# Neighbourhood attention of an encoder trunk on Trainium2: heads taken one by one, or two at a time in the halves of the TensorE array

## The chip, the cores and the metric

One core of a Trainium2 chip (trn2) runs the whole kernel. The metric is the device time of one execution in microseconds (us), median of several runs. Everything is float32. The large products are made from three matmuls in the `float32r` form (a value is cut into a high and a low part); the small products of the attention are plain float32 matmuls, each of which appears in the trace as two passes (two weight loads and two matmuls).

## What is computed

A trunk of two layers over 512 tokens of width 1024. Each layer is half a SwiGLU feed-forward step, a mixer of two groups of heads side by side, and another half feed-forward step. The part that is changed is the neighbourhood attention, eight heads of width 64 on an 8 x 64 grid of tokens:

```python
for j in range(GRID_W // COL_BLOCK):          # four blocks of 16 columns
    qb = q[:, :, :, j * COL_BLOCK:(j + 1) * COL_BLOCK]
    kb = k[:, :, :, c0:c0 + COL_SLAB][:, :, key_rows]      # 32 columns of keys
    vb = v[:, :, :, c0:c0 + COL_SLAB][:, :, key_rows]
    s = jnp.einsum('bhrqd,bhrwkd->bhrqwk', qb, kb).astype(jnp.float32) * scale
    s = s + bias[None].astype(jnp.float32)
    s = jnp.where(valid[:, None, :], s, NEG_INF)
    p = jax.nn.softmax(s.reshape(B, H, rows, COL_BLOCK, wh * COL_SLAB), axis=-1)
    outs.append(jnp.einsum('bhrqwk,bhrwkd->bhrqd', p, vb))
...
na_o = rmsnorm(merge_heads(na_o), na_gain)
```

Beside it, four heads of gated linear attention (GLA) run over the same tokens. Their outputs and those of the neighbourhood attention go through one output projection.

## The kernel before, in words

Activations lie transposed: 128 rows of features by 512 tokens per tile. A head of 64 features fills half of the 128 rows, so a pair of heads `hp` shares one tile for q and one for k. For each block `j` of 128 queries there are 256 keys.

The mixer (`mixer`, L530) is made of four streams of steps: the two GLA pairs (`gla_all`), the neighbourhood attention (`na_all`, L890) and the fillers (`fillers`, L916), which are the projections with the large weights and the first part of the output projection. `interleave` (L502) puts the steps in order by a plan: each step says how long it holds TensorE and how long its successor must wait. The order of that plan is the priority; a scheduler then takes, engine by engine, the first instruction that is ready and has its buffers, so neighbouring steps can mix.

`na_unit` (L828) is one head and two query blocks; there are 16 units in a mixer and two mixers. A unit has three steps, and `na_all` runs them staggered: in each round it begins a unit, makes the second step of the unit before and the third step of the one before that, and then waits until the planned period `NAP` = 5.46 is over.

1. Scores (L846): two matmuls of 64 rows by 256 keys, in one PSUM bank of the tag `sc`. VectorE adds the bias and takes the maximum (L851), changes its sign (L854), ScalarE makes the exponential and the sum (L855), VectorE the reciprocal (L857) and the product with it (L860). The result lies in a tile `pp`.
2. Four transposes (L864) into the PSUM bank `tp`, and a copy by ScalarE back into `pp` (L866).
3. Values (L874): four matmuls of 128 rows by 64 columns into one half, `b` to `b + 64`, of the bank `o`. After the last unit of a pair VectorE copies the bank to a tile `nao` (L879), which is split into high and low parts (`osplit`), and its squares are summed.

The bias of a head is loaded on GpSimd's DMA queue at the head's first unit (L834, L835) into two tiles `nb` of the tag `na`, which has six buffers. `pp`, `nao`, `sq` and the tiles of the row scale have the same tag.

PSUM has eight banks: four `mm` for the projections, two `sc`, which the scores of the GLA streams use as well (L623, L697, L711, L564), one `tp` and one `o`.

Of the kernel before, what the change touches and what calls it, by code (L numbers as in the profile page):

```python
# [31 lines left out]
WARM = 13  # L32
NAP = 5.46
DEPTH = 2
# [26 lines left out]
def trunk_kernel(ctx, tc, xin, wgu, wdn, win, wcode, wgate, wout, vec, rpbt,  # L61
# [42 lines left out]
    def pair(name, gain=None, src=None):  # L104
        # both parts of a tile side by side
        t = sp.tile([P, 2, T], F32R, tag="pr", name=nm(name), bufs=NPR)
        h, l = t[:, 0, :], t[:, 1, :]
        split(src, h, l, gain)
        return h, l
# [19 lines left out]

    # the tensor engine's clock comes up while the first data are on their way  # L130
    zero = cp.tile([P, P], F32, name="zero")
# [37 lines left out]

# [1 line left out]
    XC = [None] * KP  # L171
# [27 lines left out]

# [1 line left out]
    XD = [None] * KD  # L201
# [35 lines left out]
    def rsqrt_row(ps, n, t, r, a, act=False):  # L237
        # 1/sqrt(mean + eps): exp(-ln/2) as a start, then one Newton step
        S.activation(r, ps, AF.Ln, bias=epsc, scale=1.0 / n)
        S.activation(r, r, AF.Exp, scale=-0.5)  # L240
        if act:
            S.activation(t, ps, AF.Identity, bias=epsc, scale=1.0 / n)
        else:
            V.tensor_scalar(t, ps, 1.0 / n, EPS, ALU.mult, ALU.add)
        V.tensor_tensor(a, r, r, op=ALU.mult)
        V.scalar_tensor_tensor(a, a, -0.5, t, ALU.mult, ALU.mult)
        V.scalar_tensor_tensor(r, a, 1.5, r, ALU.add, ALU.mult)
        return r
# [4 lines left out]

# [1 line left out]
    pend = []  # L255
# [76 lines left out]
    def dmat_steps(pss, src, tags, raw=None, ws=None):  # L332
        # the two weight tiles straight times the chunks without row scales
        raw = raw or dload(src, nc.scalar)
        # (ws: parts that are there already, by quarter, or as a list by chunk pair)
        w = ws if isinstance(ws, list) else dict(ws or {})
        pss += [psum(tag) for tag in tags]
        for c in range(KD):
            i = c // 2
            for ps, q in zip(pss, ((1, 0), (2, 3))[c % 2]):  # L340
                if w is ws:
                    (h, l), k = w[i], q
                else:
                    if q not in w:
                        w[q] = wsplit(raw[:, q * T:(q + 1) * T])
                    (h, l), k = w[q], i
                cs = slice(k * P, (k + 1) * P)
                mm3(ps, h[:, cs], l[:, cs], *XD[c], c == 0, c == KD - 1)
            yield
# [5 lines left out]
    def ffn(l, which):  # L355
# [27 lines left out]
        def direct_pairs(hid):  # L383
            # the first weight tiles, while the row scales are on their way
            def evac(bg, bu):
# [92 lines left out]
    def last_row(pss, hs):  # L478
        # the last two chunks and the row scales of the final norm, for one half of the tokens
        sqs = [st["acc"]]  # L480
# [21 lines left out]
    def interleave(streams, got):  # L502
        # emits the streams' steps in the order in which the tensor engine can take them:
        # a step says how long it holds the engine and when its successor can follow
        now = 0.0
# [24 lines left out]
    def mixer(l):  # L530
        st["lab"] = f"M{l}"
        got = {}

        # gate codes: both parts of the weights side by side, summed by the gate product
        cd, cr = sl("cd"), sl("cr", F32R)
# [10 lines left out]
        def codes():  # L546
            # both copies of the codes; then the first as high parts, the second as low parts
            ps = psum("tp")
# [47 lines left out]
        def gla_levels(pr):  # L596
# [22 lines left out]
            def blocks(ps, op):  # L619
                # the eight blocks of 64 tokens, odd ones in the lower half of the rows  # L620
                for i in range(8):
                    o = (i % 2) * 64
                    PE.matmul(ps[o:o + 64, (i // 2) * 64:(i // 2 + 1) * 64], *op(i), start=True, stop=True)  # L623
# [157 lines left out]

        # neighbourhood attention
        def vmat_steps(pss, src, tags):
            # the values with the tokens as rows: the chunks' token blocks times two weight tiles
            raw = dload(src, nc.scalar)
# [41 lines left out]

        def na_unit(hp, hh, jp, ctxd):  # L828
            hd = 2 * hp + hh
            b = hh * 64  # L830
            q, k = got["qk", hp]
            if jp == 0:
                nb0, nb1 = sl("nb", F32, "na"), sl("nb", F32, "na")
                nc.gpsimd.dma_start(nb0, rpbt[l, hd, :, :T])  # L834
                nc.gpsimd.dma_start(nb1[:, :H2], rpbt[l, hd, :, T:])  # L835
                ctxd["nb", hd] = (nb0[:, :H2], nb0[:, H2:], nb1[:, :H2])
            nbv = ctxd["nb", hd]
            pss = psum("sc")
            pp = sl("pp", F32, "na")
            sm = small(4)  # L840
            kb = k[b:b + 64, :]
            for jj in range(2):
                j = 2 * jp + jj
                krhs = bass.AP(kb.tensor, kb.offset + KOFF[j][0],
                               [list(kb.ap[0]), [64, 2], [KOFF[j][1], 2], [1, 64]])
                PE.matmul(pss[:, jj * 256:(jj + 1) * 256], q[b:b + 64, j * P:(j + 1) * P], krhs,  # L846
                          start=True, stop=True)
            for jj in range(2):
                j = 2 * jp + jj
                cs = slice(jj * 256, (jj + 1) * 256)  # L850
                V.tensor_tensor_reduce(pp[:, cs], pss[:, cs], nbv[(0, 1, 1, 2)[j]],  # L851
                                       op0=ALU.add, op1=ALU.max, scale=1.0, scalar=-3.0e38,
                                       accum_out=sm[:, jj:jj + 1])
                V.tensor_scalar(sm[:, jj:jj + 1], sm[:, jj:jj + 1], -1.0, None, ALU.mult)  # L854
                S.activation(pp[:, cs], pp[:, cs], AF.Exp, bias=sm[:, jj:jj + 1],  # L855
                             accum_out=sm[:, 2 + jj:3 + jj])
            V.reciprocal(sm[:, 2:4], sm[:, 2:4])  # L857
            for jj in range(2):
                cs = slice(jj * 256, (jj + 1) * 256)
                V.tensor_scalar(pp[:, cs], pp[:, cs], sm[:, 2 + jj:3 + jj], None, ALU.mult)  # L860
            yield 0.9, 0.0
            pt = psum("tp")
            for i in range(4):
                PE.transpose(pt[:, i * P:(i + 1) * P], pp[:, i * P:(i + 1) * P], idn)  # L864
            pT = pp
            S.activation(pT, pt, AF.Copy)  # L866
            yield 0.5, 0.0
            if hh == 0 and jp == 0:
                ctxd["po"] = psum("o")
            po = ctxd["po"]  # L870
            for jj in range(2):
                j = 2 * jp + jj
                for c in range(2):
                    PE.matmul(po[b:b + 64, j * P:(j + 1) * P],  # L874
                              got["v", hp][VSEL[j][c]][:, hh * 64:(hh + 1) * 64],
                              pT[:, (jj * 2 + c) * P:(jj * 2 + c + 1) * P],
                              start=(c == 0), stop=(c == 1))
            if hh == 1 and jp == 1:
                V.tensor_copy(nao := sl("nao", F32, "na"), po)  # L879
                osplit(nao, hp, lvec(l, hp))  # L880
                if hp == 0:
                    st["nacc"] = sl("nacc")
                    S.activation(st["nacc"], po, AF.Square)
                else:
                    sq = sl("sq", F32, "na")
                    S.activation(sq, po, AF.Square)
                    V.tensor_tensor(st["nacc"], st["nacc"], sq, op=ALU.add)
            yield 0.9, 0.0

        def na_all():  # L890
            ctxd = {}
            act = []
            for u in range(16 + DEEP):
                if u < 16:
                    hp = u // 4
                    yield ("qk", hp)
                    yield ("v", hp)
                    act.append(na_unit(hp, (u // 2) % 2, u % 2, ctxd))
                left = NAP
                for gq in act[::-1]:  # L900
                    y = next(gq, None)
                    if y is not None:
                        left -= sum(y)
                        yield y
                act = act[-DEEP:]
                yield 0.0, max(left, 0.0)
# [132 lines left out]
def layout(a):  # L1039
# [7 lines left out]
    def quads(w, t1, t2):  # L1047
        # w: [n, 1024, cols], tiles t1, t2: first columns -> [n, P, 4 * 4 * 128]
        n = w.shape[0]
# [87 lines left out]
```

## Time and profile before

| | |
|---|---|
| median of 3 runs | 1989.24 us (1986.94 to 1990.84) |
| span of the profiled execution | 1989.2 us |
| TensorE busy | 1969.5 us (99%), weight loads 1717.5 us (86%) |
| VectorE busy | 1423.7 us (72%) |
| ScalarE busy | 1025.6 us (52%) |
| GpSimd busy | 17.5 us (1%) |
| granted TensorE clock | 0.996 of full speed |

The page begins with busy times and ends with the costliest groups of instructions. Matmuls are pipelined: a matmul's own duration (some 0.27 to 0.4 us here) is longer than the time until the next one starts. What a group of them costs is therefore read from the distance of starts in the timeline, or from the chain of waits, which counts every stretch of time once. The first mixer lies at about 362 to 644 us of the span, the second at about 1342 to 1626 us.

### The profile page before, as it was taken

Reading aid. Unit: us, or ns where it says so; the run is one execution under the profiler, and the core shown is the slowest. Engines: PE = TensorE matmul, PEld = TensorE weight load, DVE = VectorE, ACT = ScalarE, POOL = GpSimd, SP = SyncE. Lnnn points to the kernel's source line nnn. Section 1 sums busy time; section 2 is a strip of 40 time slices with the busy share of each in tenths; the row PEclk is TensorE's granted clock in tenths of the full one; section 3 lists DMA queues with packets and bytes.
Section 4 is the critical chain, followed back from the end, with each engine's and each line's share of the span. In section 5 each row is a group of like instructions: output and inputs, shape, how many; then the busy total and the mean of one; then the engine's idle time right before and its main releaser. Section 6 shows DMA issues by size and latency. Waiting matters only on the chain.

```text
span 1989.2 us, 32211 instructions
## 1 busy us (share of the span) xinstructions
PE 1969.5 (99%) x12490; PEld 1717.5 (86%) x12490; DVE 1423.7 (72%) x2745; ACT 1025.6 (52%) x1959; POOL 17.5 (1%) x36
## 2 busy tenths in 40 slices
PE   8999999999999999999999999999999999999997
PEld 7889999878778898999889898988777888999896
DVE  6958767666549985967787596775664689769585
ACT  5535535455555552644555364554554555536364
POOL 0000000000000000000000000000000000000000
PEclk9999999999999999999999999999999999999999
DMA  4332323222112332232223232223221133323322
GB/s 152 113 109 101 107 98 109 93 72 68 65 38 65 118 109 93 105 107 101 97 100 106 90 105 104 101 93 106 78 70 35 46 101 103 107 100 110 108 78 74
DMA packets 57737, 185.69 MB, mean 93 GB/s; under 512 B 6640, under 2 KB 13296, under 8 KB 45296
## 3 DMA queue, kind: packets, MB, share of 16 engines
q1 hardware_dynamic: 29904, 132.07, 19.4%
q10 hardware_dynamic: 25632, 45.27, 7.0%
q0 software_dynamic: 2048, 6.29, 1.0%
q8 instruction: 98, 1.61, 0.3%
q14 instruction: 55, 0.45, 0.1%
HBM read 181.51 MB, written 2.10 MB: 92 GB/s over the span
## 4 chain that ended last, share of the span: by engine, by line
PE 97%; DVE 1%; DMA 1%; ACT 0%; issue 0%; DVEq 0%; ACTq 0%
PE F_mm L166 14%; PE F_mm L168 14%; PE F_mm L167 14%; PE F_sc L166 9%; PE F_sc L167 9%; PE F_sc L168 9%; PE M_mm L166 6%; PE M_mm L168 6%; PE M_mm L167 6%; PE M_sc L623 2%; PE M_o L874 2%; PE M_sc L846 2%; PE M_tp L864 1%; PE M_sc L711 1%; PE M_mm L768 1%; DMA wraw<-in_wgu 0%
## 5 line engine op out<-in xcount | busy, mean ns | idle before, releaser
L146 ACT ACTIVATE F_wh<-F_wraw 128x512 fp32r<-128x512 f32 (+1 forms) x472 | 290.3, 618 | 453.7 <-PE F_sc L167 242.2
L166 PE MATMUL F_mm<-F_xc,F_wh 128*128 128x256 f32 x1792 | 500.7, 282 | 1.7 <-ACT F_wh L146 1.7
L167 PE MATMUL F_mm<-F_xc,F_wh 128*128 128x256 f32 x1792 | 501.5, 281 | 0.0
L168 PE MATMUL F_mm<-F_xc,F_wl 128*128 128x256 f32 x1792 | 495.0, 282 | 0.0
L147 DVE TENSOR_TENSOR F_wl<-F_wraw,F_wh 128x512 fp32r<-128x512 f32 (+1 forms) x472 | 313.3, 670 | 154.3 <-ACT F_wh L146 149.2
L166 PEld LDWEIGHTS F_mm<-F_xc,F_wh 128*128 128x128 f32 x1792 | 339.3, 190 | 4.3 <-ACT F_wh L146 2.5
L167 PEld LDWEIGHTS F_mm<-F_xc,F_wh 128*128 128x128 f32 x1792 | 340.3, 190 | 1.9
L168 PEld LDWEIGHTS F_mm<-F_xc,F_wl 128*128 128x128 f32 x1792 | 335.6, 190 | 0.0
L166 PE MATMUL F_sc<-F_hid,F_wh 128*128 128x512 f32 (+1 forms) x716 | 275.6, 387 | 1.3 <-DVE xt L452 1.3
L167 PE MATMUL F_sc<-F_hid,F_wh 128*128 128x512 f32 (+1 forms) x716 | 276.6, 386 | 0.0
L168 PE MATMUL F_sc<-F_hid,F_wl 128*128 128x512 f32 (+1 forms) x716 | 276.4, 386 | 0.0
L146 ACT ACTIVATE F_wh<-F_ws 128x512 fp32r<-128x512 f32 x256 | 162.3, 634 | 166.7 <-PE F_mm L167 106.9
L147 DVE TENSOR_TENSOR F_wl<-F_ws,F_wh 128x512 fp32r<-128x512 f32 x256 | 174.9, 688 | 41.8 <-ACT F_wh L146 38.6
L166 PEld LDWEIGHTS F_sc<-F_hid,F_wh 128*128 128x128 f32 x716 | 134.5, 188 | 28.9 <-DVE xt L452 3.0
L168 PEld LDWEIGHTS F_sc<-F_hid,F_wl 128*128 128x128 f32 x716 | 134.5, 188 | 26.5
L167 PEld LDWEIGHTS F_sc<-F_hid,F_wh 128*128 128x128 f32 x716 | 134.6, 188 | 25.7
L452 DVE SCALAR_TENSOR_TENSOR xt<-F_sc,xt 128x512 f32<-128x512 f32 x94 | 65.0, 692 | 97.0 <-PE F_sc L168 96.4
L166 PE MATMUL M_mm<-F_xd,M_wh 128*128 128x512 f32 x304 | 122.2, 403 | 0.0
L167 PE MATMUL M_mm<-F_xd,M_wh 128*128 128x512 f32 x304 | 120.6, 398 | 0.0
L168 PE MATMUL M_mm<-F_xd,M_wl 128*128 128x512 f32 x304 | 120.5, 397 | 0.0
L147 DVE TENSOR_TENSOR M_wl<-M_wraw,M_wh 128x512 fp32r<-128x512 f32 (+1 forms) x112 | 73.4, 668 | 36.3 <-ACT M_wh L146 23.1
L146 ACT ACTIVATE M_wh<-M_wraw 128x512 fp32r<-128x512 f32 (+1 forms) x112 | 67.7, 615 | 55.4 <-PE M_mm L167 37.6
(327 smaller groups left out, 3247.5 us busy)
## 6 DMA issues: line engine op xcount, KB each, us to landing
F_wraw<-in_wgu SPq DMA_DIRECT2D x64, 1024.0 KB, 4.8
F_wraw<-in_wdn SPq DMA_DIRECT2D x32, 1024.0 KB, 4.9
M_wraw<-in_win ACTq DMA_DIRECT2D x88, 256.0 KB, 3.6
F_wraw<-in_wgu ACTq DMA_DIRECT2D x80, 256.0 KB, 3.6
F_wraw<-in_wdn SPq DMA_DIRECT2D x16, 768.0 KB, 4.2
M_nb<-in_rpbt POOLq DMA_DIRECT2D x16, 256.0 KB, 3.0
M_wraw<-in_wout SPq DMA_DIRECT2D x16, 256.0 KB, 2.7
xt<-in_xin SPq DMA_DIRECT2D x8, 256.0 KB, 5.0
```

The lines of the kernel that those rows point to most:

```text
L146: S.activation(h, src, AF.Copy)
L147: V.tensor_tensor(l, src, h.bitcast(F32), op=ALU.subtract)
L166: PE.matmul(ps, wh, rh, start=first, stop=False, skip_group_check=more)
L167: PE.matmul(ps, wh, rl, start=False, stop=False, skip_group_check=more)
L168: PE.matmul(ps, wl, rh, start=False, stop=last, skip_group_check=more)
L452: V.scalar_tensor_tensor(xt[:, c, :], pss[j], 0.5, xt[:, c, :], ALU.mult, ALU.add)
L623: PE.matmul(ps[o:o + 64, (i // 2) * 64:(i // 2 + 1) * 64], *op(i), start=True, stop=True)
L711: PE.matmul(ps[:, j * 256:(j + 1) * 256], kk[b:b + 64, s * P:(s + 1) * P], qq[b:b + 64, o:o + 256], start=True, stop=True)
L768: PE.matmul(dst, vs(2 * half + j), fa[:, o:o + P], start=False, stop=(j == 1))
L846: PE.matmul(pss[:, jj * 256:(jj + 1) * 256], q[b:b + 64, j * P:(j + 1) * P], krhs, start=True, stop=True)
L864: PE.transpose(pt[:, i * P:(i + 1) * P], pp[:, i * P:(i + 1) * P], idn)
L874: PE.matmul(po[b:b + 64, j * P:(j + 1) * P], got["v", hp][VSEL[j][c]][:, hh * 64:(hh + 1) * 64], pT[:, (jj * 2 + c) * P:(jj * 2 + c + 1) * P],
```

## The change

The two heads of a pair are taken together: a unit is now a pair and two query blocks, eight units in a mixer. The score matmuls of the two heads alternate, one in rows 0 to 63 and one in rows 64 to 127 of the array, each head with a bank `sc` of its own. The value matmuls of the two heads alternate between output rows 0 to 63 and 64 to 127 of the bank `o`, that is, between the column halves of the array. The bias is loaded into `pp` itself, one round ahead (`na_load`), and VectorE adds it in place; it is loaded for two blocks at a time, so the middle variant is loaded twice. The sign of both maxima is changed in one instruction. The copy to `nao` is gone, and the split reads the bank `o` itself. `sq` takes a buffer of the tag `ws` in place of `na`. The planned period is 10.4 for a unit of two heads, against 5.46 for one head, and the two transposes of a unit follow each other with a planned gap of 0.3.

```diff
-NAP = 5.46
+NAP = 10.4
+NAX = 0.0
+NAT = 0.3
...
-        def na_unit(hp, hh, jp, ctxd):
-            hd = 2 * hp + hh
-            b = hh * 64
+        def na_load(hp, jp):
+            pps = []
+            for hh in range(2):
+                pp = sl("pp", F32, "na")
+                nc.gpsimd.dma_start(pp, rpbt[l, 2 * hp + hh, :, jp * H2:jp * H2 + T])
+                pps.append(pp)
+            return pps
+
+        def na_unit(hp, jp, pps, ctxd):
             q, k = got["qk", hp]
-            if jp == 0:
-                nb0, nb1 = sl("nb", F32, "na"), sl("nb", F32, "na")
-                nc.gpsimd.dma_start(nb0, rpbt[l, hd, :, :T])
-                nc.gpsimd.dma_start(nb1[:, :H2], rpbt[l, hd, :, T:])
...
-            pss = psum("sc")
-            pp = sl("pp", F32, "na")
+            sco = psum("sc"), psum("sc")
+            rows = slice(0, 64), slice(64, P)
             for jj in range(2):
                 j = 2 * jp + jj
...
-                PE.matmul(pss[:, jj * 256:(jj + 1) * 256], q[b:b + 64, j * P:(j + 1) * P], krhs,
-                          start=True, stop=True)
...
+                for hh in range(2):
...
+                    PE.matmul(sco[hh][:, jj * 256:(jj + 1) * 256], q[rows[hh], j * P:(j + 1) * P], krhs,
+                              start=True, stop=True)
...
-                V.tensor_scalar(sm[:, jj:jj + 1], sm[:, jj:jj + 1], -1.0, None, ALU.mult)
...
+                V.tensor_scalar(sm[:, 0:2], sm[:, 0:2], -1.0, None, ALU.mult)
...
+            yield 1.0, NAX
+            for pp in pps:
+                pt = psum("tp")
+                for i in range(4):
+                    PE.transpose(pt[:, i * P:(i + 1) * P], pp[:, i * P:(i + 1) * P], idn)
+                S.activation(pp, pt, AF.Copy)
+                yield 0.6, NAT
...
                 for c in range(2):
-                    PE.matmul(po[b:b + 64, j * P:(j + 1) * P],
-                              got["v", hp][VSEL[j][c]][:, hh * 64:(hh + 1) * 64],
-                              pT[:, (jj * 2 + c) * P:(jj * 2 + c + 1) * P],
-                              start=(c == 0), stop=(c == 1))
-            if hh == 1 and jp == 1:
-                V.tensor_copy(nao := sl("nao", F32, "na"), po)
-                osplit(nao, hp, lvec(l, hp))
+                    v = got["v", hp][VSEL[j][c]]
+                    for hh in range(2):
+                        PE.matmul(po[rows[hh], j * P:(j + 1) * P], v[:, rows[hh]],
+                                  pps[hh][:, (jj * 2 + c) * P:(jj * 2 + c + 1) * P],
+                                  start=(c == 0), stop=(c == 1))
+            if jp == 1:
+                osplit(po, hp, lvec(l, hp))
...
-                    sq = sl("sq", F32, "na")
+                    sq = sl("sq", F32, "ws")
...
-            yield 0.9, 0.0
+            yield 1.1, 0.0
...
+            units = []
+            pps = na_load(0, 0)
+            for u in range(8 + DEEP):
+                if u < 8:
+                    yield ("qk", u // 2)
+                    yield ("v", u // 2)
+                    units.append(na_unit(u // 2, u % 2, pps, ctxd))
+                left = NAP if u < 8 else 3.0
+                for age, n in enumerate((1, 2, 1)):
+                    if 0 <= u - age < 8:
+                        for _ in range(n):
+                            y = next(units[u - age])
+                            left -= sum(y)
+                            yield y
+                if u < 7:
+                    pps = na_load((u + 1) // 2, (u + 1) % 2)
                 yield 0.0, max(left, 0.0)
```

## Rows read from the trace of the kernel before

**Rows 1.** The page, part 1: busy us, share, instructions.

```profile
PE 1969.5 (99%) x12490; PEld 1717.5 (86%) x12490; DVE 1423.7 (72%) x2745; ACT 1025.6 (52%) x1959; POOL 17.5 (1%) x36
```

**Rows 2.** Waits of TensorE, whole span: us in total, times, longest.

```profile
PE F_mm L166 <- ACT I_wh L146: 4.1, 1, 4.1
```

**Rows 3.** Groups by line and shape, TensorE: count, busy us, mean ns.

```profile
L846 PE MATMUL M_sc<-M_k,M_q 64*128 64x256 f32 x128 | 36.1, 402 | 0.0
...
L874 PE MATMUL M_o<-M_pp,M_v 128*64 128x128 f32 x128 | 21.4, 282 | 0.0
```

**Rows 4.** Chain of waits, first mixer, in order of time: start us, us.

```profile
415.93 1.06 PE M_sc L846 x4
...
434.51 1.02 PE M_o L874 x8
...
453.92 0.91 PE M_sc L623 x30
...
539.81 1.08 PE M_sc L697 x8
...
572.97 1.64 PE M_sc L697 x16
```

**Rows 5.** Timeline of TensorE around one score cluster: start us, us.

```profile
415.53 0.28 PE L167 MATMUL M_mm<-M_wl,F_xd 128*128 128x256 f32 x1
415.65 0.28 PE L168 MATMUL M_mm<-M_wh,F_xd 128*128 128x256 f32 x1
415.86 1.13 PE L846 MATMUL M_sc<-M_k,M_q 64*128 64x256 f32 x4
416.91 0.50 PE L166 MATMUL M_mm<-F_xd,M_wh 128*128 128x512 f32 x1
417.25 0.40 PE L167 MATMUL M_mm<-F_xd,M_wh 128*128 128x512 f32 x1
417.49 0.40 PE L168 MATMUL M_mm<-F_xd,M_wl 128*128 128x512 f32 x1
```

**Rows 6.** Timeline of TensorE where scores of both kinds meet: start us, us.

```profile
534.93 0.82 PE L697 MATMUL M_sc<-M_ga 64*128 64x128 f32 x5
535.49 0.48 PE L846 MATMUL M_sc<-M_k,M_q 64*128 64x256 f32 x1
...
535.81 0.38 PE L846 MATMUL M_sc<-M_k,M_q 64*128 64x256 f32 x1
535.82 0.27 PE L697 MATMUL M_sc<-M_ga 64*128 64x128 f32 x1
536.02 0.59 PE L846 MATMUL M_sc<-M_k,M_q 64*128 64x256 f32 x2
```

**Rows 7.** The L874 weight loads: duration ns min/median/max, first and last start.

```profile
L874 PEld LDWEIGHTS M_o<-M_pp,M_v x128: 132/137/137, 434.4 to 1540.0; 128*64 128x64 f32 x128
```

**Rows 8.** Stretches, first mixer: length; busy PE, PEld, DVE, ACT, POOL; clock; DMA.

```profile
440.00:480.00 40.00, 40.00 (x398) 32.51 (x399) 29.52 (x100) 22.87 (x55) 2.69 (x5) 1.00 0.16 51
...
600.00:640.00 40.00, 40.00 (x209) 34.19 (x209) 35.52 (x61) 19.53 (x36) 0.00 (x0) 1.00 0.21 70
```

**Rows 9.** Groups by line and shape, VectorE: count, busy us, mean ns, idle before.

```profile
L851 DVE CUSTOM_DVE_ANT_0 M_pp<-M_sc,M_nb 128x256 f32<-128x256 f32 x64 | 24.6, 422 | 35.4 <-PE M_sc L846 35.4
...
L854 DVE TENSOR_SCALAR M_sm<-M_sm 128x1 f32<-128x1 f32 x64 | 8.2, 148 | 0.0
L879 DVE COPY M_nao<-M_o 128x512 f32<-128x512 f32 x8 | 5.5, 687 | 15.6 <-PE M_o L874 15.6
```

**Rows 10.** Groups by line and shape, ScalarE and GpSimd: count, busy us, mean ns, idle.

```profile
L855 ACT ACTIVATE M_pp<-M_pp,M_sm 128x256 f32<-128x256 f32 x64 | 31.9, 501 | 21.4 <-DVE M_sm L854 21.2
L866 ACT ACTIVATE M_pp<-M_tp 128x512 f32<-128x512 f32 x32 | 19.0, 595 | 29.2 <-PE M_tp L864 28.9
...
L834 POOL DMA_DIRECT2D M_nb<-in_rpbt x16 | 8.7, 546 | 1441.5 <-PE F_mm L168 1111.9 <-DVE M_pp L860 210.3 <-DVE M_sm L851 62.5
```

**Rows 11.** The page, part 6, DMA issues: count, KB each, median us to landing.

```profile
M_nb<-in_rpbt POOLq DMA_DIRECT2D x16, 256.0 KB, 3.0
```

More of the change, by code (lines that the diff above doesn't have):

```diff
@@ L826, in post_qk @@
             return post
-        def na_unit(hp, hh, jp, ctxd):
-            hd = 2 * hp + hh
-            b = hh * 64
-            q, k = got["qk", hp]
-            if jp == 0:
-                nb0, nb1 = sl("nb", F32, "na"), sl("nb", F32, "na")
-                nc.gpsimd.dma_start(nb0, rpbt[l, hd, :, :T])
-                nc.gpsimd.dma_start(nb1[:, :H2], rpbt[l, hd, :, T:])
-                ctxd["nb", hd] = (nb0[:, :H2], nb0[:, H2:], nb1[:, :H2])
-            nbv = ctxd["nb", hd]
-            pss = psum("sc")
-            pp = sl("pp", F32, "na")
-            sm = small(4)
-            kb = k[b:b + 64, :]
+        def na_load(hp, jp):
[5 more added lines that the diff above has]
+            return pps
@@ L842, in na_unit @@
+        def na_unit(hp, jp, pps, ctxd):
+            q, k = got["qk", hp]
+            sco = psum("sc"), psum("sc")
+            rows = slice(0, 64), slice(64, P)
             for jj in range(2):
                 j = 2 * jp + jj
-                krhs = bass.AP(kb.tensor, kb.offset + KOFF[j][0],
-                               [list(kb.ap[0]), [64, 2], [KOFF[j][1], 2], [1, 64]])
-                PE.matmul(pss[:, jj * 256:(jj + 1) * 256], q[b:b + 64, j * P:(j + 1) * P], krhs,
-                          start=True, stop=True)
@@ L848, in na_unit @@
[L848 to L853, printed above, removed]
-                V.tensor_scalar(sm[:, jj:jj + 1], sm[:, jj:jj + 1], -1.0, None, ALU.mult)
-                S.activation(pp[:, cs], pp[:, cs], AF.Exp, bias=sm[:, jj:jj + 1],
-                             accum_out=sm[:, 2 + jj:3 + jj])
@@ L857, in na_unit @@
[L857 to L860, printed above, removed]
-            yield 0.9, 0.0
[L862 to L868, printed above, removed]
+                for hh in range(2):
+                    kb = k[rows[hh], :]
+                    krhs = bass.AP(kb.tensor, kb.offset + KOFF[j][0],
+                                   [list(kb.ap[0]), [64, 2], [KOFF[j][1], 2], [1, 64]])
+                    PE.matmul(sco[hh][:, jj * 256:(jj + 1) * 256], q[rows[hh], j * P:(j + 1) * P], krhs,
+                              start=True, stop=True)
@@ new lines, in na_unit @@
+            halves = slice(0, H2), slice(H2, T)
+            sms = []
+            for ps, pp in zip(sco, pps):
+                sm = small(4)
+                for jj, cs in enumerate(halves):
+                    V.tensor_tensor_reduce(pp[:, cs], ps[:, cs], pp[:, cs],
+                                           op0=ALU.add, op1=ALU.max, scale=1.0, scalar=-3.0e38,
+                                           accum_out=sm[:, jj:jj + 1])
+                V.tensor_scalar(sm[:, 0:2], sm[:, 0:2], -1.0, None, ALU.mult)
+                for jj, cs in enumerate(halves):
+                    S.activation(pp[:, cs], pp[:, cs], AF.Exp, bias=sm[:, jj:jj + 1],
+                                 accum_out=sm[:, 2 + jj:3 + jj])
+                sms.append(sm)
@@ new lines, in na_unit @@
+            for sm, pp in zip(sms, pps):
+                V.reciprocal(sm[:, 2:4], sm[:, 2:4])
+                for jj, cs in enumerate(halves):
+                    V.tensor_scalar(pp[:, cs], pp[:, cs], sm[:, 2 + jj:3 + jj], None, ALU.mult)
+            yield 1.0, NAX
[5 more added lines that the diff above has]
+                yield 0.6, NAT
@@ L869, in na_unit @@
+            if jp == 0:
                 ctxd["po"] = psum("o")
@@ L884, in na_unit @@
                 else:
-                    sq = sl("sq", F32, "na")
+                    sq = sl("sq", F32, "ws")
                     S.activation(sq, po, AF.Square)
                     V.tensor_tensor(st["nacc"], st["nacc"], sq, op=ALU.add)
-            yield 0.9, 0.0
+            yield 1.1, 0.0
         def na_all():
             ctxd = {}
[L892 to L905, printed above, removed]
+            units = []
[14 more added lines that the diff above has]
+                    pps = na_load((u + 1) // 2, (u + 1) % 2)
                 yield 0.0, max(left, 0.0)
```

## The prediction, made before the changed kernel was run

> **What bounds the kernel now.** I read the page first. TensorE is busy 99% of the span, VectorE 72%, ScalarE 52% [rows 1]. A modelled busy time can hide gaps, so the waits of TensorE come next. The largest of six groups is one single wait of 4.1 us, at the very start of the program [rows 2]. [...] Any time that the change takes off TensorE's queue is a gain in the first instance. The question is how much it takes off, and whether the other engines keep up afterwards.
>
> What do the heads cost now? The count of records [rows 3] gives 128 score passes, four to a unit, so 32 clusters, and 128 value passes with `v`, as many again with the shifted tile `vm`, eight to a unit, so 32 clusters too. The chain of waits prices a cluster of four score passes at 1.06 us and one of eight value passes at 1.02 us [rows 4]. Both stream 1024 columns, so a lone tile costs about 1.0 us per 1000 columns. The group means (402 and 282 ns [rows 3]) would be the wrong price, since pipelined passes overlap.
>
> Does the array run two half tiles at once? The trace already has the answer for both directions. GLA scores (L623) go to 64 rows by 64 columns and alternate between the column halves. Thirty passes take 0.91 us [rows 4]; that is 1920 columns, 0.47 us per 1000, where one tile alone needs 1.0. For the row halves there is a meeting of two lines: L846 starts at 535.49, 535.81, 536.02, while L697, begun at 534.93, still starts passes at 535.82 in the other row half [rows 6]. The distance from 535.81 to 536.02 is 0.21, the pace at which four passes fit into 1.06 us. So neither slows the other. Also, eight L697 passes alone take 1.08 us, and sixteen, the second eight in the other row half, 1.64 instead of 2.1 [rows 4]; only the middle ones overlap there, because the halves do not alternate. The change makes them alternate.
>
> **The change part by part.**
>
> *Scores, two heads side by side.* 32 clusters of 1.06 us become 16 that take as long as one did. Saved: 16 x 1.06 = 17.0 us. Lower bound nothing, if the passes do not meet.
>
> *Values in column halves.* 32 clusters of 1.02 us become 16. Saved: 16 x 1.02 = 16.3 us. A form of 128 rows with both column halves at once does not occur in the trace. The nearest row is L623, where both halves of the columns read the same rows; I take its full overlap. Lower bound nothing.
>
> [...] A lone value stream hides its weight loads of 137 ns [rows 7]: eight passes in 1.02 us are 128 ns each [rows 4], shorter than the load. [...] Sixteen bare loads of 137 ns are 2.2 us, more than the two old clusters (2.04), and the value part would save nothing. L623, with the same rows and other columns at 0.47 us per 1000 [rows 4], is against it, so I keep 16.3 and give bare loads a small chance below.
>
> *Switches of the tile form.* Ahead of a score cluster the distance of starts is 0.21 in place of the usual 0.12; after it 0.34 in place of 0.24 [rows 5]. A cluster between wide matmuls thus pays 0.19 us more than its own passes. 32 clusters go, so at most 6.1 us, and nothing where a cluster stands between other small ones. I take half, 3.0 us.
>
> *Two banks at once.* A unit now wants both `sc` banks, which GLA scores use as well. If only one is free, the scheduler may take head 0 first and head 1 later, and the overlap is lost for that unit, 1.06 us each. Bounds: 0 and 16 units, 17 us. Emission order often puts a unit between the two score steps of a GLA level, so I take 5 units, 5.3 us lost. [...]
>
> *Transposes.* Their number stays. But the two heads' transposes now follow each other through the one bank `tp`, and the second four wait for ScalarE's copy of the first, 595 ns [rows 10]. The plan puts a projection step between; if ScalarE takes the copy at once, nothing is lost, and if it first makes two exponentials of 501 ns [rows 10], 1.6 us a unit, 25.6 in all. The scheduler can fill with projections, and TensorE does not wait today, so I take 1 us.
>
> *VectorE.* Of 64 sign changes at 148 ns 32 go, 4.7 us, and eight copies of 687 ns, 5.5 us [rows 9]. It gains 10 us, and none of it counts, as VectorE does not end the stage. The addition in place has the shape it had (422 ns [rows 9]), and I count it at no difference. If it, or the split that now reads PSUM, were slower by a tenth, that is 2.5 us on an engine with room: 29.5 of 40 us in the densest attention stretch. If the stretch shrinks by a tenth, that is 82%. The tightest stretch is the output projection, 35.5 of 40 us [rows 8], which the change does not touch, though it comes sooner; what is late next is the GLA tail there. `sq` goes to `ws`, whose buffers GLA gates and the output step share; I count nothing.
>
> *Bias.* Loads go from 384 to 512 KB a head, on GpSimd's queue and 16 DMA engines that are busy a fifth of the time (0.16 and 0.21 [rows 8]). An issue is 546 ns [rows 10], landing 3.0 us [rows 11]. They are made a round ahead, as soon as the values of two units earlier have freed the buffers, so 4.1 us must fit into about eight planned us. Nothing else is queued on GpSimd behind them. Behind VectorE's first addition, which waits for them, stand weight splits, and TensorE would wait for those. Bounds 0 and 16 x 4.1 us; I take 0.
>
> **Sum.** 17.0 + 16.3 + 3.0 - 5.3 - 1.0 = 30.0 us. The profiled span is 1989.2 and the median of the runs 1989.24, so nothing is to be added: 1959.
>
> **The rivals.**
>
> *Scores do not meet.* The two-bank condition fails nearly always, or the row halves take turns. Values 16.3 and half the switches remain, less 1 for the transposes: 16.8 us, giving 1972. For it: only two `sc` banks. Against: the meeting of L846 and L697 at full pace [rows 6]. Chance 0.15.
>
> [...] Chance 0.04.
>
> *The turn through* `tp`. TensorE waits for ScalarE's copies: 36.3 - 25.6 = 10.7 us, about 1978.5, and with the lost score overlap 1984. Chance 0.10, half of it within 0.2% of before.
>
> *Slower: the bias comes late.* The load starts only when the third-last unit frees its buffers. If VectorE stands still for the whole of issue and landing of both tiles, 2 x 0.546 + 3.0 = 4.1 us, and TensorE behind it, 16 units cost 65.5 us: 1989.2 - 36.3 + 65.5 = 2018. It outweighs the gain from 36.3 / 16 = 2.3 us a unit. Against it: today's loads are issued in the unit that uses them, and L851 waits for TensorE alone [rows 9]. Chance 0.07.
>
> **How the numbers follow.** The forecast has 0.64. All switches and no loss would be 39.4 us, 1949.8, the low end. The high end takes in the first two rivals and stands at 1978; range 1949 to 1978. About 0.2% (4 us) is what can be told from no change. Faster: 0.64 + 0.15 + 0.04 + 0.05 = 0.88; within: 0.05; slower: 0.07.
>
> **What would show it.** After: L846 clusters of eight passes in about 1.07 us and L874 clusters of sixteen in about 1.03, starts in pairs some ns apart; 16 of each. Score clusters of four with 1.06 mean that the banks did not allow it; a value cluster of 2 us that the column halves take turns. Waits of TensorE that name L866 are the `tp` turn, waits of L851 for a DMA the late bias. The prediction is wrong if TensorE's waits in the mixers grow past a few us, or if both mixers do not shrink by some 15 us each.

## The result, and the profile after

The changed kernel takes 1977.77 us (median of 4 runs, 1977.57 to 1978.87), the kernel before, run beside it, 1989.39 us. The ratio is 0.9945, with an interval of 0.9932 to 0.9958. It is faster by 11.6 us, where 30.0 were forecast: in the direction and inside the range, but little over a third of the gain.

The profiled execution after took 1977.83 us, its span is 1976.1 us. Page, part 1, which answers to [rows 1]:

```profile
PE 1955.6 (99%) x12490; PEld 1704.4 (86%) x12490; DVE 1418.0 (72%) x2705; ACT 1023.2 (52%) x1959; POOL 17.4 (1%) x36
```

TensorE is as full as before, with the same number of instructions, and its waits (us in total, times, longest) are still small:

```profile
PE F_mm L168 <- ACT I_wh L148: 4.0, 3, 3.2
...
PE M_mm L168 <- ACT M_oh L151: 1.2, 2, 0.6
```

Inside the mixers the largest sum is 1.2 us. So the missing 18 us are not in a new wait; they must be in TensorE's own queue. The scores are now L850, the transposes L873, the values L884. The chain of waits of the first mixer, L850 and L884 only (start us, us, count), answers to [rows 4]:

```profile
413.50 1.06 PE M_sc L850 x8
...
424.99 1.06 PE M_sc L850 x4
...
430.30 1.06 PE M_sc L850 x4
...
445.36 1.02 PE M_o L884 x16
...
447.28 1.06 PE M_sc L850 x4
...
450.07 1.06 PE M_sc L850 x4
...
461.68 1.06 PE M_sc L850 x4
...
464.39 0.58 PE M_o L884 x6
464.97 1.06 PE M_sc L850 x4
466.03 0.80 PE M_o L884 x10
```

This is the finding in ten rows. The first unit's scores are what was forecast: eight passes of two heads in the 1.06 us that four took before. Then every cluster has **four** passes and still takes 1.06: one head alone, as before the change. The rest of the first mixer has eight more of these, and the second mixer the same pattern: 2 units of 16 have their heads side by side, 14 have not. The first value unit also does what was forecast, sixteen passes in 1.02; the second is cut into six and ten, with scores between, and takes 0.58 + 0.80 = 1.38.

Why are they apart? The timeline of TensorE around unit 2 (start us, us, operation, tiles, shapes):

```profile
424.28 0.70 PE L625 MATMUL M_sc<-M_ga,M_kt 64*64 64x64 f32 x16
424.92 1.13 PE L850 MATMUL M_sc<-M_k,M_q 64*128 64x256 f32 x4
425.97 0.66 PE L873 MATMUL M_tp<-con,M_pp 128*128 128x128 f32 x4
...
430.23 1.13 PE L850 MATMUL M_sc<-M_k,M_q 64*128 64x256 f32 x4
...
431.72 0.46 PE L625 MATMUL M_sc<-M_ga,M_kt 64*64 64x64 f32 x8
```

Just ahead of head 0 stand GLA scores (L625), which write to the same two banks `sc`. Head 0 starts, head 1 follows 5.3 us later. The compiled program's own order of instructions on TensorE says the same with names: the two heads of unit 1 alternate, those of unit 2 stand eighteen rows of this listing apart. (The first number is the row, in which equal neighbours share a place, `x2` or `x4`; the one behind `M_sc` is that of the tile, that is, of the bank's user.)

```
2421 L850 MATMUL M_sc_4334<-M_k_4023,M_q_4022 128x256
2422 L850 MATMUL M_sc_4335<-M_k_4023,M_q_4022 128x256
2423 L850 MATMUL M_sc_4334<-M_k_4023,M_q_4022 128x256
2424 L850 MATMUL M_sc_4335<-M_k_4023,M_q_4022 128x256
...
2468 L850 MATMUL M_sc_4437<-M_k_4023,M_q_4022 128x256 x2
2469 L873 MATMUL M_tp_4461<-con,M_pp_4089 128x128 x4
...
2486 L850 MATMUL M_sc_4438<-M_k_4023,M_q_4022 128x256 x2
```

The scheduler takes each instruction when its buffer is free, so two matmuls written side by side need not run so. That the banks are what splits them is tested below.

**Accounts.** To see where time goes in a full queue, I summed over the first mixer the distance from each matmul pass's start to the next start in the timeline, by kind of the earlier one (us). "Pieces" are unbroken stretches of a kind. The mixer runs from its first matmul to the first feed-forward matmul behind its last one. "Projections" holds the few 512-wide matmuls of the neighbouring steps that fall into this time. In the column e3 about 17 us of the mixer ran at a granted clock of 0.50; see there.

| | before | after | e2 | e3 | e4 | e5 | e8 | e11 |
|---|---|---|---|---|---|---|---|---|
| scores | 16.50 | 15.87 | 15.87 | 10.90 | 14.83 | 12.03 | 10.62 | 15.87 |
| values | 16.86 | 10.98 | 14.84 | 13.36 | 8.19 | 8.19 | 9.41 | 11.14 |
| transposes | 9.28 | 7.70 | 7.55 | 9.79 | 7.28 | 7.65 | 7.03 | 7.76 |
| projections 128x512 | 179.06 | 180.87 | 180.76 | 180.42 | 182.17 | 178.97 | 179.55 | 181.87 |
| their pieces | 44 | 50 | 53 | 43 | 52 | 34 | 50 | 54 |
| GLA scores 64x64 | 18.91 | 19.39 | 19.77 | 18.82 | 20.91 | 18.11 | 20.46 | 20.24 |
| mixer 1 | 300.4 | 295.2 | 299.9 | 296.7 | 294.3 | 286.9 | 286.6 | 297.5 |
| mixer 2 | 302.0 | 296.5 | 301.0 | 296.5 | 296.9 | 285.8 | 286.6 | 297.8 |

The mixers gained 5.2 + 5.5 = 10.7 us, and this is what the traces show of the change. The spans differ by 13.1; the other 2.4 lie ahead of the first mixer, in code that did not change. Near the start of the program the granted TensorE clock was 0.50 for some 6.8 us of the execution before, and 1.00 over the same stretch of the one after (stretch; length; busy PE, PEld, DVE, ACT, POOL; clock; DMA):

```profile
10.00:20.00 10.00, 6.73 (x18) 5.32 (x19) 6.67 (x11) 7.36 (x14) 0.00 (x0) 0.66 0.64 222
10.00:20.00 10.00, 7.28 (x29) 5.26 (x30) 6.97 (x12) 7.67 (x14) 0.00 (x0) 1.00 0.62 214
```

It fell at about 11.8 us, while TensorE stood idle for the 4.1 us of [rows 2] (9.2 to 13.3 us); after, the longest piece of that wait is 3.2 us. The first mixer starts at 348.3 us before, and at 345.0 to 346.6 in the other traces of the table. Twice the first mixer's differences between before and after: scores 2 x 0.63 = 1.3, values 2 x 5.88 = 11.8, transposes 3.2 gained; projections 3.6 and GLA scores 1.0 lost.

The other engines. VectorE's groups (count, busy us, mean ns, idle before and what ended it), beside [rows 9]:

```profile
L857 DVE CUSTOM_DVE_ANT_0 M_pp<-M_sc,M_pp 128x256 f32<-128x256 f32 x64 | 24.4, 421 | 21.9 <-PE M_sc L850 21.7
...
L860 DVE TENSOR_SCALAR M_sm<-M_sm 128x2 f32<-128x2 f32 x32 | 5.3, 167 | 0.7
```

The bias loads in the page's part 6 (count, KB each, median us to landing), beside [rows 11]:

```profile
M_pp<-in_rpbt POOLq DMA_DIRECT2D x32, 256.0 KB, 3.2
```

The addition in place costs 421 ns where it cost 422, waits for TensorE alone and never for a load: the bias is early. A sign change of two columns takes 167 ns in place of twice 148.

### The profile page after: what moved, and what is told of

The parts are those of the page before. It is cut to its first block, busy times and chain, and to the rows that moved or that the text cites. A ratio compares the mean times of both kernels' runs of the same rounds, so it can differ in the third digit from the quotient of the medians.

```text
span 1976.1 us, 32194 instructions
## 1 busy us (share of the span) xinstructions
PE 1955.6 (99%) x12490; PEld 1704.4 (86%) x12490; DVE 1418.0 (72%) x2705; ACT 1023.2 (52%) x1959; POOL 17.4 (1%) x36
## 4 chain that ended last, share of the span: by engine, by line
PE 96%; DMA 1%; DVE 1%; ACT 1%; issue 0%; SPq 0%; DVEq 0%; ACTq 0%
PE F_mm L168 14%; PE F_mm L170 14%; PE F_mm L169 14%; PE F_sc L168 9%; PE F_sc L170 9%; PE F_sc L169 9%; PE M_mm L168 6%; PE M_mm L169 5%; PE M_mm L170 5%; PE M_sc L625 2%; PE M_sc L850 2%; PE M_o L884 1%; PE M_tp L873 1%; PE M_sc L713 1%; PE M_mm L770 1%; DMA OP_wraw<-in_wout 1%
```

## The experiments

The theory formed on these rows: the shared `sc` banks split the pairs; give the pairs their banks together, and the forecast comes true. (From e6 on the expectations call it theory B.) Rivals were that alternation itself is worth little, that broken value clusters are the larger loss, and that the copy taken from VectorE matters. Eleven kernels ran beside the kernel before, whose medians were then 1989.0 to 1990.3 us. All edits are against the changed kernel.

| run | median us | ratio to before | interval |
|---|---|---|---|
| the change | 1977.77 | 0.9945 | 0.9932 to 0.9958 |
| e1 scores by head | 1978.55 | 0.9949 | 0.9937 to 0.9962 |
| e2 values by head | 1987.33 | 0.9993 | 0.9984 to 1.0002 |
| e3 hold both banks | 1979.61 | 0.9953 | 0.9940 to 0.9965 |
| e4 values whole | 1976.72 | 0.9941 | 0.9928 to 0.9955 |
| e5 = e3 + e4 | 1959.14 | 0.9848 | 0.9835 to 0.9862 |
| e6 three `sc`, three `mm` | 1983.89 | 0.9969 | 0.9956 to 0.9981 |
| e8 scores in `mm` banks | 1960.38 | 0.9854 | 0.9841 to 0.9868 |
| e8 + e4 | 1962.70 | 0.9867 | 0.9852 to 0.9882 |
| e10 = e8 + e1 | 1962.35 | 0.9864 | 0.9849 to 0.9879 |
| e11 copy put back | 1984.10 | 0.9972 | 0.9961 to 0.9982 |
| e9 one `sc`, one `mm`, + e4 | 1962.82 | 0.9867 | 0.9854 to 0.9881 |

### e1: the scores' alternation undone

```diff
-            for jj in range(2):
-                j = 2 * jp + jj
-                for hh in range(2):
+            for hh in range(2):
+                for jj in range(2):
+                    j = 2 * jp + jj
```

> The changed kernel with one edit: the four score matmuls of a unit are issued head by head instead of alternating. Theory (the alternation is lost already, because a unit seldom finds both sc banks free; the trace after shows 15 of 16 units' scores as two clusters of four passes at 1.06 us): nothing but the first unit of each mixer can lose, at most 2 x 1.06 us, so 1977.8 to 1980. Rival (the scores do run side by side and the missing gain went elsewhere): the score part comes back, 15 units of 1.06 us, about 1993.

Measured 1978.55 us, within the spread of the change: alternating the scores brought nothing as it stands. (The heads of 14 units are apart, one unit of each mixer has them together; the expectation says 15.) The chain of e1 holds a surprise in its first unit:

```profile
414.09 1.07 PE M_sc L850 x8
...
425.58 1.06 PE M_sc L850 x4
```

Head by head, the eight passes still take 1.07 us. The second head's first pass starts 13 ns after the first head's first, though the four passes of the first head stand ahead of it in the compiled order: here a pass for the free half of the array began with the pass four places ahead of it.

### e2: the values' alternation undone

```diff
-            for jj in range(2):
-                j = 2 * jp + jj
-                for c in range(2):
-                    v = got["v", hp][VSEL[j][c]]
-                    for hh in range(2):
+            for hh in range(2):
+                for jj in range(2):
+                    j = 2 * jp + jj
+                    for c in range(2):
+                        v = got["v", hp][VSEL[j][c]]
```

> The changed kernel with one edit: the eight value matmuls of a unit are issued head by head instead of alternating. Theory (nearly the whole gain is the column halves: value passes take 11.0 us a mixer after and 16.9 before): 2 x 5.9 us come back, about 1989.5. Rival (the gain comes from the other edits, the copy that is gone, fewer sign changes, the new period): the time stays near 1978.

Measured 1987.33 us: 9.6 us over the change, close to the whole gain. So what the change brought came from the values. Chain of e2, its first value unit:

```profile
444.73 1.51 PE M_o L884 x16
```

Not 2.04, as two heads in turn would give, and not 1.02. So the loss was smaller than the 11.8 us expected, and the timeline of the same unit shows why: four passes of head 0 start alone, then those with `vm` (head 0) and with `v` (head 1) start in pairs, and `vm` of head 1 is alone at the end.

```profile
444.66 0.65 PE L884 MATMUL M_o<-M_pp,M_v 128*64 128x128 f32 x4
445.15 0.27 PE L884 MATMUL M_o<-M_pp,M_vm 128*64 128x128 f32 x1
445.15 0.32 PE L884 MATMUL M_o<-M_pp,M_v 128*64 128x128 f32 x1
445.26 0.27 PE L884 MATMUL M_o<-M_pp,M_vm 128*64 128x128 f32 x1
445.31 0.27 PE L884 MATMUL M_o<-M_pp,M_v 128*64 128x128 f32 x1
...
445.64 0.60 PE L884 MATMUL M_o<-M_pp,M_vm 128*64 128x128 f32 x4
```

Head 1 begins when four of head 0's eight passes are left. Four places ahead of their turn is also what e1 shows, and the sixteen L697 passes that take 1.64 us instead of 2.1 in [rows 4] fit it: by an estimate from eight alone in 1.08, 0.135 a step, four alone, four pairs and four alone are twelve steps, 1.62. A score head has four passes, and the order made no difference there (1.07 us against 1.06); a value head has eight, and it did (1.51 against 1.02).

### e3: no head starts before both banks are free

```diff
+            mark = PE.matmul(sco[1][:, :1], q[rows[1], :P], k[rows[1], :1], start=True, stop=True)
...
-                    PE.matmul(sco[hh][:, jj * 256:(jj + 1) * 256], q[rows[hh], j * P:(j + 1) * P], krhs,
-                              start=True, stop=True)
+                    with tc.issue_after(mark.ins):
+                        mark = PE.matmul(sco[hh][:, jj * 256:(jj + 1) * 256], q[rows[hh], j * P:(j + 1) * P],
+                                         krhs, start=True, stop=True)
```

A matmul of one column claims the second bank first (its result is overwritten), and the score matmuls are chained behind it.

> The changed kernel with one edit: a score matmul of one column takes the second sc bank first, and the four real score matmuls are queued one behind the other behind it, so that they can only start when both banks are held. Theory (two banks are what parts the heads): scores fall from 15.9 to about 8.5 us a mixer plus some 1 to 2 us for the extra small passes and their switches, 5 to 7 us less a mixer, 1964 to 1968. Rival (a unit that holds both banks makes the GLA scores wait, and TensorE with them): TensorE's waits grow by as much, 1977 or more.

Measured 1979.61 us: a miss, though the scores did meet. In the accounts the scores fall by 5.0 us a mixer, and values (+2.4), transposes (+2.1) and the 256-wide matmuls of GLA (8.3 to 11.5) take 7.7. Chain of e3 (the scores are L852; L713 are the 256-wide matmuls of GLA, which no edit touches):

```profile
430.80 1.06 PE M_sc L852 x8
...
556.45 3.71 PE M_sc L713 x8
```

The same GLA matmuls in the chain of the changed kernel:

```profile
554.41 1.92 PE M_sc L713 x8
```

In e3 the same eight passes take almost twice as long. The stretches of e3 give the reason (length; busy PE, PEld, DVE, ACT, POOL; clock; DMA):

```profile
550.00:555.00 5.00, 3.00 (x48) 2.43 (x48) 5.00 (x16) 4.99 (x15) 0.00 (x0) 0.89 0.33 103
...
560.00:565.00 5.00, 5.00 (x14) 3.36 (x14) 0.00 (x0) 1.84 (x4) 0.00 (x0) 0.50 0.00 0
```

The granted TensorE clock fell to 0.50 for 17.1 us of each mixer (553.9 to 571.0 us in the first), and the mean clock of all five executions is 0.989 or 0.990, where the changed kernel has 0.997 to 0.999. In the 5 us in which it fell TensorE stood idle for 2.0, in two waits; the first was for ScalarE to empty an `sc` bank (L702). Waits of TensorE in e3, both mixers together:

```profile
PE M_mm L168 <- ACT M_oh L151: 3.4, 2, 1.8
PE M_sc L625 <- ACT M_am L702: 2.5, 2, 1.3
...
PE M_o L886 <- ACT M_pp L876: 1.2, 2, 0.8
```

An estimate from 1.92 and 3.71: the 17.1 us would have taken about 8.8 at the full clock, so the clock cost some 8 us a mixer and 16 in all. Without it e3 would stand near 1963, about where the theory had put it (1964 to 1968). So holding the banks does pay; it makes TensorE wait for a bank late in the mixer (1.2 and 1.3 us), and the larger part of the price was the clock that fell around these waits. No run has the same order at the full clock, so this stays an estimate.

### e4: the values in one piece

```diff
+            with tc.high_priority():
+                mark = None
...
-                    for hh in range(2):
-                        PE.matmul(po[rows[hh], j * P:(j + 1) * P], v[:, rows[hh]],
+                        for hh in (1, 0):
+                            with tc.issue_after(mark.ins) if mark else ExitStack():
+                                mark = PE.matmul(po[rows[hh], j * P:(j + 1) * P], v[:, rows[hh]],
```

> The changed kernel with one edit: the eight value matmuls of a unit are queued one behind the other, the head whose copy comes last first, and with high priority, so that nothing is put between them. Theory (the value part fell short of 8.2 us a mixer because score matmuls are put into the middle of it, which leaves passes without a partner): values fall from 11.0 to 8.2 us a mixer, 2 x 2.7 us, about 1972. Rival (the column halves do not overlap fully even in one piece): 1977 to 1978.

Measured 1976.72 us, a miss for the expected 1972. The values fall to 8.19 a mixer, 1.02 a unit, which is what the forecast had; but projections (+1.3) and GLA scores (+1.5) rise, cut into more pieces.

### e5: both together

> The edits of e3 (both sc banks taken before the scores) and e4 (values in one piece, with priority) together. e3 brought the scores down from 15.9 to 10.9 us a mixer and gave it all back: value and transpose clusters were cut up (plus 2.4 and 2.1 us) and TensorE waited some 3.5 us a mixer. Theory A (the cutting up was the larger part, and e4 removes it for the values): about 4 us a mixer less than the changed kernel, 1968 to 1972. Theory B (two banks are too few for GLA and pairs together, whatever the order; what is won in the scores comes back as waits and switches): 1975 to 1980.

Measured 1959.14 us, 18.6 below the change, where e3 and e4 alone stood at +1.8 and -1.1. Chain of e5 (the values are L889, the claiming matmul L844):

```profile
429.69 1.06 PE M_sc L852 x8
...
435.95 1.02 PE M_o L889 x16
...
451.00 0.31 PE M_sc L844 x2
...
454.85 1.06 PE M_sc L852 x8
```

All value clusters are whole and 10 of the 16 score clusters, and the projections run in 34 pieces instead of 50. The expectation took e3's losses for clusters that were cut up; most of them, by that estimate, were the clock. In e5 TensorE has no wait over 0.5 us where e3 has the two, and the granted clock stays at 1.00 in both mixers. With the clock's 16 us taken off e3, the two edits come to about 15 + 1 us, and e5 has 18.6: they nearly add. Whether it is e4's order that keeps the clock up was not tested.

### e6: a third `sc` bank, taken from the projections

```diff
-MMB = 4
+MMB = 3
```

> The changed kernel with one edit: three sc banks and three mm banks in place of two and four. Theory B (banks part the heads): without any forced order most score pairs stay whole, scores fall from 15.9 to about 11 us a mixer, and if the projections can do with three banks the time is 1967 to 1971. Rival (the projections need their four banks): the scores fall all the same, but TensorE waits for evictions of mm, 1978 or more.

Measured 1983.89 us. More units are whole with one more bank (12 of 16, scores 10.2 us a mixer), so the banks were the limit; but the feed-forward step, which uses the `mm` banks over the whole span, pays for it. Waits of e6:

```profile
PE F_mm L168 <- ACT F_o L299: 11.2, 16, 0.7
PE M_mm L168 <- ACT M_oh L151: 5.5, 2, 2.7
```

### e8: the scores in two `mm` banks

```diff
-            sco = psum("sc"), psum("sc")
+            sco = psum("mm"), psum("mm")
```

> The changed kernel with one edit: the two score banks of a unit are taken from the four mm banks; sc is left to the GLA scores. Theory B: the scores no longer meet the GLA scores in the bank pool, most pairs stay whole, scores about 10.7 us a mixer, 5 us a mixer less, 1967 to 1970. Rival (projections wait for the banks that the scores hold): TensorE's waits or pieces grow by as much, 1976 or more.

Measured 1960.38 us (1960.05 to 1961.76), 17.4 below the change by one line. Order, tiles and work are those of the change; only the banks that the pair draws from are others, and free more often. Chain of e8:

```profile
414.18 1.06 PE M_mm L850 x8
...
426.11 1.06 PE M_mm L850 x8
...
441.40 1.06 PE M_mm L850 x8
...
447.50 1.02 PE M_o L884 x16
...
458.09 1.06 PE M_mm L850 x8
...
465.09 1.02 PE M_o L884 x16
```

12 of the 16 score units are whole in the program's order, against 2, and 10 of the 16 value units, against 2. No wait inside the mixers is among TensorE's largest. The scores came out as expected (10.62 us a mixer), the time 7 us below the range: values, projections and transposes, which the expectation did not count, gave 3.1, 2.6 and 1.3 us in both mixers together. This is the plainest evidence that the shared banks undid the change.

### e8 with e4, and e10: what is left

> The edits of e8 and of e4 together: scores in mm banks, values in one piece with priority. Theory B: scores about 9.6 us a mixer (15.9 in the changed kernel), values 8.2 (11.0), together 9 us a mixer less, 1960 to 1966, near the time forecast for the change itself. Rival (what is saved returns as waits or as more pieces of other work): 1970 or more.

> The edits of e8 (scores in mm banks) and e1 (scores issued head by head) together, so the banks are free but the four score matmuls do not alternate. Theory C (TensorE starts a matmul for a free row half up to four passes ahead of its turn; in e1 the one whole unit of a mixer took 1.07 us head by head, as when alternating): as e8, 1960 to 1962, and the alternation in the code is worth nothing for scores. Rival (halves meet only when their matmuls alternate): 10 whole units lose 1.06 us each a mixer or a part of that, 1965 to 1973.

With whole values 1962.70, with the scores head by head 1962.35 (their edits are those of e4 and e1). Both lie some 2 us above e8 with overlapping intervals. Held values gain 1.2 us a mixer on their own account (9.41 to 8.20) and lose it in the order: TensorE now waits 3.5 us for the weights of the output step. In e10 the scores' account is 10.66 us a mixer, against 10.62 in e8. Chain of e10:

```profile
415.91 1.07 PE M_mm L850 x8
...
427.85 1.07 PE M_mm L850 x8
```

Where both banks were free, the two heads ran side by side without any alternation in the program, eight passes in 1.07 us as in e1.

### e11: the copy put back

```diff
-                osplit(po, hp, lvec(l, hp))
+                V.tensor_copy(nao := sl("nao", F32, "ws"), po)
+                osplit(nao, hp, lvec(l, hp))
```

> The changed kernel with one edit undone: the bank o is again copied by VectorE and the split reads the copy, eight copies of 687 ns. Step of the prediction (what VectorE gains counts for nothing): within 2 us of 1977.8. Rival (VectorE does end the stage somewhere): up to 5.5 us more, 1983.

The copy takes its buffer from `ws`, though; before, it came from `na`. Measured 1984.10 us (1981.38 to 1985.67), 6.3 over the change by the medians, 5.4 by the ratios: a miss, and about the rival's figure. Eight copies of VectorE, 5.5 us in [rows 9], cost about as much as if they stood on the path. No wait of TensorE has grown, though:

```profile
PE F_mm L168 <- ACT I_wh L148: 3.9, 3, 3.2
...
PE M_mm L168 <- ACT M_oh L151: 1.1, 2, 0.6
```

What moved is the order: 54 pieces of projections instead of 50, both mixers longer (+2.3 and +1.3). That is the whole of what the profiled execution has more (1981.39 against 1977.83), but it is one of the two shortest of seven. The rest, some 2 us, stays open. So does what moved the order: VectorE's time, the buffer from `ws`, or the moment at which the bank `o` comes free. No run parts the three.

### e9: one bank of each kind

```diff
-            sco = psum("sc"), psum("sc")
+            sco = psum("sc"), psum("mm")
```

The edit of e4 is made as well.

> A candidate: one score bank of a unit from sc and one from mm, values in one piece with priority. Theory B: a unit competes for one bank of each kind, so most pairs stay whole, as in e8; between e5 and e8 with values whole, 1958 to 1963. Rival (any claim on sc parts the pairs as in the changed kernel): 1970 or more.

Measured 1962.82 us: it is enough that the two heads don't wait for two of the banks that GLA keeps busy. No version beat e5 and e8 clearly; these two stand 18.6 and 17.4 us below the change.

## Why the prediction was wrong, by its steps

The forecast had 30.0 us in three parts. Beside them the accounts of the first mixer, doubled, and as the rest what the two mixers together gained or lost beyond these:

| | forecast | after | e8 |
|---|---|---|---|
| scores, with the loss at the banks | 17.0 - 5.3 = 11.7 | 1.3 | 11.8 |
| values | 16.3 | 11.8 | 14.9 |
| the rest: switches, transposes, order | 3.0 - 1.0 = 2.0 | -2.4 | 2.5 |
| both mixers | 30.0 | 10.7 | 29.2 |

**The step that failed is "Two banks at once".** It named the mechanism and the place, and took 5 of 16 units, 5.3 us; 14 of 16 lost the overlap, 14.8 us at its own price, and the scores gained 1.3 us instead of 11.7. The size came from the emission order, where units often stand between two GLA steps. It should have come from the banks: GLA scores are taken by the scheduler whenever a bank is free, two banks serve the GLA streams and both heads, and the plan has no term for needing both. e8 shows it by itself: other banks, nothing else in the code, and the scores give what was forecast (there 4 of 16 units are still apart, close to the 5 of the forecast). So the rival "Scores do not meet", in its first form, is what happened, and it had a chance of 0.15. Its price for the scores was about right; that the time is 1977.8 and not its 1972 comes from the next two steps. That the time lies within the range, just under its end of 1978, is due to the room left for the first two rivals; the forecast itself was missed. (The sum also took span and time as one measure; after, an execution's span is 1.7 us shorter than its time, little beside the miss.)

**Values: right in mechanism, off in size.** Sixteen passes in 1.02 us where nothing comes between, so L623 in [rows 4] was the right row to go by. But in the change most clusters are cut after six passes by scores or GLA work that got its bank, 0.58 + 0.80 = 1.38 us, and at the end of each piece two passes run without a partner (starts 464.59 and 464.70, 466.45 and 466.56): 4.5 us less than forecast. The 8.19 in e4 are 17.3 us saved in both mixers, so the 16.3 were there to be had; e2 shows that alternation was needed here (1.51 us a unit without it).

The rival that the loads of the value weights lie bare (chance 0.04; the forecast without the values' 16.3, 1975.5) fell: no run shows bare loads. Weight loads, and the cluster that they feed:

```profile
L884 PEld LDWEIGHTS M_o<-M_pp,M_v x128: 133/136/137, 445.3 to 1538.2; 128*64 128x64 f32 x128
```

Sixteen loads of 136 ns would be 2.2 us bare; the unit takes 1.02 (chain above), less than half of that. So the loads of these column halves, which share their rows, did not lie bare.

**Switches** were to give 3.0. The clusters did not become fewer as assumed, since the scores stayed apart and the values were cut, and the projections stand in 50 pieces instead of 44, 3.6 us more. The number of pieces alone does not set that price: e8 has 50 as well and pays 1.0 us. What the switches by themselves gave is not shown.

**Transposes** were to lose 1.0 and gained 3.2, for a reason that no run looks for; no wait of TensorE names the copy (L874), so the rival of the turn through `tp` fell. **Bias** was right at nothing: no wait for a load. **VectorE** is in doubt: "none of it counts, as VectorE does not end the stage" looks at waits alone. In e11 eight copies, 5.5 us, move the end by 5.4 to 6.3 us without a longer wait of TensorE, through the scheduler's order; whether VectorE's time or the copy's buffer does it is not parted.

The statement of what would show it served well: "Score clusters of four with 1.06 mean that the banks did not allow it" is what the chain says, row after row. So does its last sign: the mixers shrank by 5.2 and 5.5 us, not by some 15 each.

## What to carry to other kernels

A pair that is to run side by side needs all its resources at one moment: count who else draws from the same banks, and if they are shared, give the pair others before anything else (here one word, worth 17.4 us). Look at the order of the compiled program, not at the order of the source: a scheduler that takes what is ready can pull a pair apart, as it did with 14 of 16 units here. Where an engine is full and nobody waits, lost time shows in the accounts by kind. And before an account is read as work that was cut up, look at the granted clock of the same stretch: in e3 it hid some 16 us, by the estimate there.

## What the hardware did that was not expected

TensorE started matmul passes for a free half of the array ahead of their turn, up to four places in these runs. Eight score passes head by head take 1.07 us, as many as alternating (e1, e10), the second head starting 13 ns after the first; sixteen value passes head by head take 1.51, between 1.02 and 2.04 (e2). For passes in different halves, these starts are not in the program's order.

The granted clock fell to 0.50 for 17.1 us in each mixer of e3, around two waits of TensorE, of 1.2 and 0.8 us in the first mixer and of 1.3 and 0.4 in the second. Eight L713 passes then took 3.71 us; in the changed kernel they took 1.92.

Two heads in the two row halves always wrote to two banks here; no run put them in one, so what that would do was not shown. Both column halves did write into one bank: those of L623, thirty passes in 0.91 us [rows 4], and those of the values, sixteen passes in 1.02.
